# A two-group encoder on one Trainium2 core: a new clock for two interleaved threads, a fixed count of gathered rows ahead of a chain, and a contiguous scatter operand

## The chip, the cores and the metric

The kernel runs on one core of a Trainium2 chip. The metric is the device time of one execution in microseconds (us), lower is better. Engines are named as in the profile: PE (matmuls), DVE (vector), ACT (activations), POOL (which issues the gathers), SP (which issues the weight loads).

## The reference

Two request groups ("prompt" and "sample", 256 tokens each, 1024 features) go through the same two layers. Layer 0 mixes with a three-group attention, layer 1 with a short convolution. Behind the mixer each layer has the PEER channel mixer, which dominates the time:

```python
def block(xc):                                   # 128 tokens
    q = (xc @ w_query).reshape(C, PEER_HEADS, 2, PEER_HALF)
    s = jnp.einsum('chpk,hpnk->chpn', q, sub_keys)
    sv, si = lax.top_k(s, PEER_TOPK)             # 16 of 128 keys, twice
    ...                                          # 16 best of 256 pairs -> eidx, 8 heads x 16
    g = jax.nn.softmax(fv, axis=-1)
    u = u_tab[eidx]                              # rows of a 16384 x 1024 table
    h = jax.nn.gelu(jnp.einsum('chkd,cd->chk', u, xc))
    return jnp.einsum('chk,chkd->cd', (g * h), v_tab[eidx])
...
x = layer_norm(ALPHA * x + f, ln2_gain[i], ln2_bias[i])
x = x + jax.nn.sigmoid(x @ ple_w_gate[i]) * (p[i] @ ple_w_proj[i])
```

## The kernel before

Each group has a generator ("thread"): `thread_a` for the prompt, `thread_b` for the sample. Each `yield` hands back a cost; the thread with the smaller clock runs next, and its clock sets the priority of what it emits (sample's clock starts at `T0B`). A scheduler then writes one instruction order per engine from these priorities and from its own estimates of durations. On the chip every engine goes through its order from front to back, so an instruction that waits holds up all behind it on its engine.

The two groups do PEER in two ways. The prompt **gathers**: for each of 2 token tiles, 8 heads and 16 picks, one indirect DMA fetches 128 rows of the table u (`gather`, L472, issued by POOL), and DVE multiplies them with x and sums (L489); then the same for table v (L510). That is 512 such row tiles a layer ("rows" below), in a ring of 8 buffers (`GB`). When the last row of tile 1 is in, DVE adds the residual and normalises (`done`), PE transposes the result (`transpose_x`, L139), and the gate (`ple`) follows, then the prompt's next layer.

The sample goes **densely** through all 16384 experts: 64 pairs of blocks, for each a load of 1 MB of u (`dense_u`, L528), 16 matmuls `hid`, a gelu on ACT (L556), a product with the gate matrix G on DVE (`hs`, L557), 1 MB of v (L559) and 8 matmuls `out` (L102). For the first 8 pairs (`pre`) `hid` is done ahead, during the sample's routing. G is built by `scatter`, in 8 chunks of 16 blocks: DVE compares (L587) and multiplies (L589) to one-hot rows I0 in float16, and PE multiplies them with the float8 matrix J, one small matmul a token (L596 in chunk 0, L603 in the others).

The sample's chain from its routing to the end of chunk 0 is kept free of rows: `hold[0]` is set when the sample's routing starts (L803), and the prompt then emits no row until chunk 0 is emitted; the next 16 rows' DVE work stands behind the last L589 of that chunk.

Of the kernel before, what the change touches and what calls it, by code (L numbers as in the profile page):

```python
# [46 lines left out]
def encoder_trunk(ctx: ExitStack, tc: tile.TileContext, A: dict):  # L47
# [11 lines left out]
    n_ = [0]  # L59
    hold = [False, None, 0]  # L60

# [22 lines left out]
    iota = T(cp, [P, NC_], "iota")  # L84
    iota16 = T(cp, [P, CH, 2 * TG], "iota16", F16)
    iotaj = T(cp, [P, NK // 4], "iotaj", F16)
# [45 lines left out]

    def transpose_x(e, x, xt, natural=False):
        for t in range(NT):
            for half in range(2):
                pt = e.tr([4, P])
                for j in range(4):
                    kc = half * 4 + j
                    nc.tensor.transpose(pt[:, j], x[t][:, kc * P:(kc + 1) * P], ident)  # L139
# [49 lines left out]
    def attention(e, g, x):  # L189
# [13 lines left out]
        def project(hp):  # L203
            base = (hp // 2) * 9 + (0 if hp % 2 == 0 else 5)
            qkT = T(ap, [P, NG, 4, S], "qkT", bufs=2)
            for gr in range(NG):
                ps = token_major(e, xt, "w_qkv", base + gr)
                for t in range(NT):
# [13 lines left out]
                    nc.scalar.activation(qkT[:, gr, :, t * P:(t + 1) * P], pt, AF.Copy)  # L222
                yield 11
            v01 = T(ap, [P, NT, 2, 2, HD], "v01", bufs=2)
            ps = token_major(e, xt, "w_qkv", base + 3)
            for t in range(NT):
                nc.scalar.activation(v01[:, t].rearrange("p a b d -> p (a b d)"), ps[t], AF.Copy)
            yield 11
            if hp % 2 == 0:
                v2 = T(ap, [P, NT, 4, HD], "v2", bufs=2)  # L230
                ps = token_major(e, xt, "w_qkv", base + 4)
                for t in range(NT):
                    nc.scalar.activation(v2[:, t].rearrange("p a d -> p (a d)"), ps[t], AF.Copy)
                yield 11
            else:
# [3 lines left out]
        def attend(hp):  # L239
# [35 lines left out]
            for hh in range(2):  # L275
                for t in range(NT):
                    held.append((hh, t, scores(hh, t)))
                    if len(held) > AHEAD:
                        values(*held.pop(0))
                    yield 2.5  # L280
            for z in held:
# [22 lines left out]
        out_proj(e, x, ot, "w_out", (ps, steps))  # L304
        yield 22

# [168 lines left out]
    def peer_gather(i, x, sel, done):  # L475
# [6 lines left out]
        def up(t, h):  # L482
            dots = T(sp, [P, TOPK], "dots", bufs=2)
            for k in range(TOPK):
                while hold[0]:
                    yield 1.0
                r = gather(u, index(t, h * TOPK + k))
                with held():
# [8 lines left out]
        def down(t, h):  # L497
# [3 lines left out]
            for k in range(TOPK):  # L501
                while hold[0]:
                    yield 1.0
                r = gather(v, index(t, h * TOPK + k))
                c = cf[:, k:k + 1]
# [38 lines left out]
    def peer_dense(e, i, xt, sel, spill, newx, pre):  # L544
# [32 lines left out]
        def scatter(c):  # L577
# [3 lines left out]
            for tg in range(S // TG):  # L581
                ts = slice(tg * TG, (tg + 1) * TG)
                if tg % 2 == 0:
                    t2 = slice(tg * TG, (tg + 2) * TG)
                    I1 = T(dp, [P, CH, 2 * TG], "I1", F16, bufs=1)
                    I0w = T(dp, [P, 2 * CH * 2 * TG], "I0", F16, bufs=2).rearrange("p (q a b) -> p q a b", q=2, a=CH)
                    nc.vector.tensor_tensor(I1, iota16, ic[:, t2].unsqueeze(1).to_broadcast([P, CH, 2 * TG]), op=ALU.is_equal)  # L587
                    bc = [P, 2, CH, 2 * TG]
                    last = nc.vector.tensor_tensor(I0w, I1.unsqueeze(1).to_broadcast(bc), gT[:, :, t2].unsqueeze(2).to_broadcast(bc), op=ALU.mult)  # L589
                I0 = I0w[:, :, :, (tg % 2) * TG:(tg % 2 + 1) * TG]  # L590
                ps = T(e.phid, [P, 512], "hid").rearrange("p (a q b) -> p a q b", q=2, b=CH)
                gv = G[:, :, ts]
                if c < SCU:
                    for k in range(TG):
                        for q in range(2):
                            nc.tensor.matmul(ps[:, k, 0], J[:, tg * TG + k], I0[:, q, :, k], start=q == 0, stop=q == 1)  # L596
                    nc.scalar.activation(gv, ps[:, :, 0].rearrange("p a b -> p b a"), AF.Copy)
                    if tg == S // TG - 1:
                        hold[:] = [False, last.ins, 2 * GB]
                    yield G  # L600
                    continue
                for k in range(TG):
                    nc.tensor.matmul(ps[:, k], J[:, tg * TG + k], I0[:, :, :, k], start=True, stop=True)  # L603
                nc.scalar.activation(gv, ps[:, :, 0].rearrange("p a b -> p b a"), AF.Copy)  # L604
# [33 lines left out]
    def ple(e, g, i, x, which):  # L638
# [4 lines left out]
        if which:  # L643
            norms(e, which, i, x)
        xt = transpose_x(e, x, e.xt())
        for nb in range(2):
# [93 lines left out]

    GCOST = 6.0
    T0B = 280.0
    RCOST = 21.0
    PM = -10000.0
# [34 lines left out]
    def thread_b():  # L779
# [4 lines left out]
        for i in range(DEPTH):  # L784
# [55 lines left out]
def _layout(inputs):  # L840
# [84 lines left out]
```

## Time and profile before

| | us |
|---|---|
| median of 3 runs (lowest to highest) | 3628.53 (3628.45 to 3635.97) |
| the profiled execution, its own time | 3627.66 |
| span of its instructions | 3625.9 |
| around the span | 1.8 |

Mean granted TensorE clock 0.955 of full speed. Busy shares are averages over stages with different limits; the stages are read from windows and waits further down.

### The profile page before, as it was taken

How to read it: one execution, taken by the hardware profiler on the slowest of the kernel's cores; microseconds unless marked ns; L12 is line 12 of the kernel's file. 1: busy time of each engine (PE TensorE's matmuls, PEld its weight loads, DVE VectorE, ACT ScalarE, POOL GpSimd, SP SyncE). 2: the span in 40 equal slices, each digit the busy share in tenths (PEclk: the TensorE clock that was granted, in tenths of full speed). 3: DMA queues.
4: the chain of work that ended last, by engine and by line, in shares of the span. 5: the costliest groups of instructions: out<-in, count | busy, mean ns of one | idle time of the engine just before them, and what ended most of it. 6: DMA issues, size and time to landing. Idle time of an engine off the chain costs nothing. (4 is left out here: it accounts for less than half of the span.)

```text
span 3625.9 us, 42260 instructions
## 1 busy us (share of the span) xinstructions
PE 3335.0 (92%) x15472; PEld 2229.4 (61%) x15472; DVE 2197.1 (61%) x4766; ACT 554.6 (15%) x1374; POOL 1400.5 (39%) x1476
## 2 busy tenths in 40 slices
PE   9998999988699999999999859895999999999967
PEld 4555555567366677667666647584566676666633
DVE  0002796047977777777741265468877777676683
ACT  1222223223100001000001112122000001000001
POOL 0110574000355555555620041000655555555660
PEclk9999999989699999999999979996999999999988
DMA  6433797333499999999974565442999999999993
GB/s 213 136 117 128 276 347 269 116 131 128 170 363 376 382 378 378 376 379 378 393 304 142 165 211 176 142 142 80 370 364 380 385 378 375 377 374 372 405 410 124
DMA packets 243568, 1007.14 MB, mean 278 GB/s; under 512 B 27553, under 2 KB 28961, under 8 KB 210593
## 3 DMA queue, kind: packets, MB, share of 16 engines
q0 software_dynamic: 147456, 536.94, 39.1%
q1 hardware_dynamic: 87264, 448.83, 34.2%
q10 hardware_dynamic: 8640, 18.68, 1.4%
q8 instruction: 122, 2.00, 0.2%
q14 instruction: 86, 0.70, 0.1%
HBM read 999.09 MB, written 5.24 MB: 277 GB/s over the span
## 5 line engine op out<-in xcount | busy, mean ns | idle before, releaser
L472 POOL DMA_INDIRECT g<-in_u_dram,ei x512 | 640.3, 1251 | 531.5 <-DVE g L489 201.1
L102 PE MATMUL out<-ur,hs 128*128 128x512 f32 x1824 | 811.6, 598 | 31.1 <-ACT k L653 28.1
L102 PE MATMUL hid<-bx1T,ur 128*128 128x256 f32 x3584 | 800.8, 382 | 11.5 <-DVE G L605 11.4
L472 POOL DMA_INDIRECT g<-in_v_dram,ei x512 | 625.7, 1222 | 424.4 <-DVE acc L510 164.1
L102 PEld LDWEIGHTS hid<-bx1T,ur 128*128 128x128 f32 x3584 | 682.3, 192 | 129.2 <-issue 26.8
L510 DVE SCALAR_TENSOR_TENSOR acc<-g,cf,acc 128x1024 f32<-128x1024 f32 x508 | 651.8, 1283 | 46.5 <-DMA g<-in_v_dram,ei 34.9
L489 DVE SCALAR_TENSOR_TENSOR g<-g,xa 128x1024 f32<-128x1024 f32 x512 | 605.9, 1223 | 47.3 <-DMA g<-in_u_dram,ei 46.5
L102 PEld LDWEIGHTS out<-ur,hs 128*128 128x128 f32 x1824 | 342.5, 192 | 417.1 <-issue 383.2
L102 PE MATMUL mm<-raw,x 128*128 128x512 f32 x1280 | 568.1, 595 | 10.1 <-DMA x<-in_xT_dram 8.1
L102 PEld LDWEIGHTS mm<-raw,x 128*128 128x128 f32 x1280 | 237.3, 191 | 272.5 <-issue 267.9
L557 DVE SCALAR_TENSOR_TENSOR hs<-hs,G 128x512 f32<-128x512 f32 x112 | 77.8, 694 | 315.8 <-ACT hs L556 315.8
L250 DVE SCALAR_TENSOR_TENSOR k<-tr,mask 128x512 f32<-128x512 f32 x32 | 22.0, 687 | 401.9 <-PE tr L247 401.9
L603 PEld LDWEIGHTS <-J 128*128 128x128 fp8e4 x3584 | 216.7, 113 | 53.7 <-issue 40.3
L102 PE MATMUL out<-bx1T,ur 128*128 128x256 f32 x1024 | 231.8, 388 | 17.0 <-ACT k L369 11.0
L603 PE MATMUL hid<-I,J 128*128 128x32 f16 x3584 | 229.5, 233 | 6.0 <-DVE G L605 6.0
L102 PEld LDWEIGHTS out<-bx1T,ur 128*128 128x128 f32 x1024 | 198.3, 195 | 47.1 <-ACT k L369 13.5
L556 ACT ACTIVATE hs<-hid 128x512 f32<-128x512 f32 x112 | 66.9, 597 | 1038.6 <-PE hid L102 1038.5
L400 POOL TENSOR_TENSOR ci<-sif 128x32 f32<-128x32 f32 x64 | 17.4, 292 | 534.9 <-ACT sif L386 533.2
L102 PE MATMUL out<-ur,x 128*128 128x512 f32 x448 | 207.2, 619 | 12.2 <-DVE x L557 12.2
L214 POOL TENSOR_TENSOR rm<-k,rope 128x128 f32<-128x128 f32 x48 | 26.1, 544 | 432.4 <-ACT k L210 432.2
L589 DVE TENSOR_TENSOR I<-I,gT 128x1024 f16<-128x1024 f16 x128 | 88.4, 691 | 135.0 <-PE hid L603 125.8
L604 ACT ACTIVATE G<-hid 128x256 f32<-128x256 f32 x224 | 85.9, 383 | 528.1 <-PE hid L603 527.8
(182 smaller groups left out, 2641.5 us busy)
## 6 DMA issues: line engine op xcount, KB each, us to landing
ur<-in_uT_dram SPq DMA_DIRECT2D x128, 1024.0 KB, 8.2
ur<-in_vp_dram SPq DMA_DIRECT2D x128, 1024.0 KB, 8.2
raw<-in_w_qkv_dram SPq DMA_DIRECT2D x144, 512.0 KB, 4.4
raw<-in_w_q_dram SPq DMA_DIRECT2D x32, 512.0 KB, 3.7
ur<-in_w_q_dram SPq DMA_DIRECT2D x32, 512.0 KB, 3.5
raw<-in_c_in_dram SPq DMA_DIRECT2D x24, 512.0 KB, 3.6
ur<-in_c_in_dram SPq DMA_DIRECT2D x24, 512.0 KB, 3.6
raw<-in_w_out_dram SPq DMA_DIRECT2D x16, 512.0 KB, 4.3
```

What stands on the lines that cost most here:

```text
L102: nc.tensor.matmul(out, a, b, start=first, stop=last)
L214: nc.gpsimd.tensor_tensor(m1, st[:, :, :2 * RH], c, op=ALU.mult)
L250: nc.vector.scalar_tensor_tensor(prf, sc, SCALE, mask[:, t], op0=ALU.mult, op1=ALU.add)
L400: eng.tensor_tensor(dst[:, :, off:off + n], src[:, :, 1, 0:n], src[:, :, 0, a0:a0 + 1].to_broadcast([P, 2, n]), op=ALU.add)
L472: nc.gpsimd.indirect_dma_start(out=t, out_offset=None, in_=tab, in_offset=bass.IndirectOffsetOnAxis(ap=idx, axis=0))
L489: nc.vector.scalar_tensor_tensor(r, r, 1.0, x[t], op0=ALU.mult, op1=ALU.mult, accum_out=dots[:, k:k + 1])
L510: nc.vector.scalar_tensor_tensor(acc[t], r, c, acc[t], op0=ALU.mult, op1=ALU.add)
L556: nc.scalar.activation(hs, hid, AF.Gelu)
L557: nc.vector.scalar_tensor_tensor(hs, hs, 1.0 / GSC, G[:, 2 * pr:2 * pr + 2], op0=ALU.mult, op1=ALU.mult)
L589: last = nc.vector.tensor_tensor(I0w, I1.unsqueeze(1).to_broadcast(bc), gT[:, :, t2].unsqueeze(2).to_broadcast(bc), op=ALU.mult)
L603: nc.tensor.matmul(ps[:, k], J[:, tg * TG + k], I0[:, :, :, k], start=True, stop=True)
L604: nc.scalar.activation(gv, ps[:, :, 0].rearrange("p a b -> p b a"), AF.Copy)
```

## The change

Five edits. (1) Rows ahead of the sample's chain: the flag is replaced by a count. A layer's first `CAP[i]` rows (170 in layer 0, 100 in layer 1) may be emitted whenever the prompt's clock says so; all further ones wait until chunk 0 of that layer's scatter is emitted. (2) The costs that the threads yield: `T0B` 280 to 420, `RCOST` 21 to 26, `GCOST` 6.0 to 5.2, the attention's projections 11 to 17, its score steps 2.5 to 5, its end 22 to 35. (3) The prompt's gate transposes start with tile 1, and those of tile 0 stand behind the first of tile 1. (4) I0 and I1 are laid out with the 16 block indices innermost, so the scatter matmul's moving operand is 32 neighbouring float16 values instead of 32 values that lie 64 bytes apart; DVE's second inputs (`ic`, `gT`) are then broadcast along the innermost axis instead of an outer one. (5) The iota constant follows that layout.

```diff
-    hold = [False, None, 0]
+    hold = [0, None, 0]
+    rows = [0]
...
-    iota16 = T(cp, [P, CH, 2 * TG], "iota16", F16)
+    iota16 = T(cp, [P, 2 * TG, CH], "iota16", F16)
...
-        for t in range(NT):
+        lead = None
+        for t in reversed(range(NT)) if late else range(NT):
...
+                    with tc.issue_after(lead) if lead is not None and t == 0 else nullcontext():
+                        ins = nc.tensor.transpose(pt[:, j], x[t][:, kc * P:(kc + 1) * P], ident)
+                    if late and lead is None:
+                        lead = ins.ins
...
-                yield 11
+                yield PCOST
...
-                while hold[0]:
+                while rows[0] >= CAP[i] and hold[0] <= i:
                     yield 1.0
+                rows[0] += 1
...
-                    nc.vector.tensor_tensor(I1, iota16, ic[:, t2].unsqueeze(1).to_broadcast([P, CH, 2 * TG]), op=ALU.is_equal)
-                    bc = [P, 2, CH, 2 * TG]
-                    last = nc.vector.tensor_tensor(I0w, I1.unsqueeze(1).to_broadcast(bc), gT[:, :, t2].unsqueeze(2).to_broadcast(bc), op=ALU.mult)
+                    nc.vector.tensor_tensor(I1, iota16, ic[:, t2].unsqueeze(2).to_broadcast([P, 2 * TG, CH]), op=ALU.is_equal)
+                    bc = [P, 2 * TG, 2, CH]
+                    last = nc.vector.tensor_tensor(I0w, I1.unsqueeze(2).to_broadcast(bc), gT[:, :, t2].rearrange("p q b -> p b q").unsqueeze(3).to_broadcast(bc), op=ALU.mult)
...
-                    nc.tensor.matmul(ps[:, k], J[:, tg * TG + k], I0[:, :, :, k], start=True, stop=True)
+                    nc.tensor.matmul(ps[:, k].rearrange("p q b -> p (q b)"), J[:, tg * TG + k], I0[:, k].rearrange("p q a -> p (q a)"), start=True, stop=True)
...
-        xt = transpose_x(e, x, e.xt())
+        xt = transpose_x(e, x, e.xt(), late=not e.deep)
...
-    GCOST = 6.0
-    T0B = 280.0
-    RCOST = 21.0
+    CAP = (170, 100)
+    GCOST = 5.2
+    T0B = 420.0
+    RCOST = 26.0
+    PCOST = 17.0
...
-            hold[0] = True
```

Where the new order differs, in three places. First DVE at the end of the sample's attention in layer 0 (`y` is the sample's state, `lnst`/`lnmv` its layer norm, `g` a gathered row, `xa` the prompt's state). Before:

```order
L187 SCALAR_TENSOR_TENSOR y_427_1681<-y_427_1681,mm_3840 128x512
L160 BN_STATS lnst_3940<-y_427_1681 128x6
L187 SCALAR_TENSOR_TENSOR y_427_1681<-y_427_1681,mm_3868 128x512
L160 BN_STATS lnst_3940<-y_427_1681 128x6
L161 BN_AGGR lnmv_3939<-lnst_3940 128x2
L174 SCALAR_TENSOR_TENSOR y_427_1681<-y_427_1681,lnmv_3939,raw_3935 128x1024
```

The same place in the changed kernel (L495 is the old L489):

```order
L192 SCALAR_TENSOR_TENSOR y_365_1413<-y_365_1413,mm_4107 128x512
L495 SCALAR_TENSOR_TENSOR g_4172,dots_4147<-g_4172,xa_5_98 128x1024
L165 BN_STATS lnst_4216<-y_365_1413 128x6 x2
L495 SCALAR_TENSOR_TENSOR g_4175,dots_4147<-g_4175,xa_5_98 128x1024
L495 SCALAR_TENSOR_TENSOR g_4178,dots_4147<-g_4178,xa_5_98 128x1024
L166 BN_AGGR lnmv_4215<-lnst_4216 128x2
```

Rows now stand between the steps of the sample's layer norm; in DVE's whole order 76 rows stood ahead of it before, and now 152 do, with 18 more between its first and the routing's first instruction.

Second, PE at the gate transposes of the prompt's tile 1 in layer 0 (`av`), inside the sample's dense stage. Before:

```order
L102 MATMUL out_5121<-ur_12232,hs_12229 128x512
L139 MATMUL av_10684<-ident_75,xa_6_99 128x128 x4
L139 MATMUL av_10690<-ident_75,xa_6_99 128x128 x2
L102 MATMUL out_5118<-ur_12444,hs_12441 128x512
L102 MATMUL out_5119<-ur_12444,hs_12441 128x512
```

Changed (L142 is the old L139, L611 the old L603):

```order
L611 MATMUL hid_10762<-I_2208_10759,J_5416 128x32
L142 MATMUL av_9482<-ident_75,xa_6_99 128x128 x4
L142 MATMUL av_9488<-ident_75,xa_6_99 128x128 x4
L611 LDWEIGHTS J_5416
L611 MATMUL hid_10781<-I_2208_10759,J_5416 128x32
```

They moved forward from the last pair of the dense stage to its middle, between two scatter groups. Counted in the order from the first matmul of chunk 0 to these transposes, PE now has 512 matmuls of 16 columns, 1392 of 32, 576 of 256 and 344 of 512; before 512, 1792, 896 and 504. In layer 1 it has 512, 1664, 704 and 416; before 512, 1792, 896 and 516.

Third, PE at the start of the prompt's convolution in layer 1 (`av<-x,raw` 128x256). Before:

```order
L139 MATMUL av_10956<-ident_75,xa_6_99 128x128 x4
L102 MATMUL av_10968<-x_10928,raw_10969 128x256 x8
L102 MATMUL av_10981<-x_10928,raw_10982 128x256 x8
L102 MATMUL av_11000<-x_10928,raw_11001 128x256 x8
L102 MATMUL av_11088<-x_10928,raw_11089 128x256 x8
```

Changed:

```order
L142 MATMUL av_9766<-ident_75,xa_6_99 128x128 x4
L103 MATMUL hid_11842<-bx1T_4244,ur_11843 128x256 x4
L103 MATMUL av_9778<-x_9738,raw_9779 128x256 x4
L103 MATMUL hid_11842<-bx1T_4244,ur_11843 128x256 x3
L103 MATMUL av_9778<-x_9738,raw_9779 128x256 x4
L103 MATMUL av_9791<-x_9738,raw_9792 128x256 x8
```

The convolution stood behind the sample's dense matmuls and now stands among them (`hid<-bx1T,ur`).

## Rows read from the trace of the kernel before

**Rows 1.** The page: span, busy time of each engine, and the DMA's GB/s over 40 slices of 90.6 us.
```profile
span 3625.9 us, 42260 instructions
...
PE 3335.0 (92%) x15472; PEld 2229.4 (61%) x15472; DVE 2197.1 (61%) x4766; ACT 554.6 (15%) x1374; POOL 1400.5 (39%) x1476
...
GB/s 213 136 117 128 276 347 269 116 131 128 170 363 376 382 378 378 376 379 378 393 304 142 165 211 176 142 142 80 370 364 380 385 378 375 377 374 372 405 410 124
```

**Rows 2.** Waits of PE over the whole span: instruction waiting, who ended the wait, total us, times, longest.
```profile
PE av L139 <- DVE xa L175: 55.5, 2, 45.0
PE hid L459 <- DVE k L449: 41.0, 2, 20.8
PE hid L596 <- DVE I L589: 39.7, 2, 19.8
PE out L102 <- ACT k L653: 28.1, 1, 28.1
PE av L102 <- ACT k L369: 13.8, 1, 13.8
```

**Rows 3.** Stretches: length, busy us of PE, PEld, DVE, ACT, POOL (instructions), granted clock, DMA share, GB/s.
```profile
587.00:757.00 170.00, 157.77 (x547) 85.65 (x546) 40.56 (x81) 45.78 (x103) 19.93 (x45) 0.98 0.35 113
...
1100.00:1800.00 700.00, 697.77 (x3553) 485.30 (x3552) 507.42 (x735) 67.79 (x153) 405.79 (x329) 1.00 0.98 380
...
2560.00:2600.00 40.00, 40.00 (x206) 21.57 (x204) 32.03 (x47) 3.07 (x8) 28.32 (x23) 1.00 1.02 410
...
2700.00:3300.00 600.00, 597.77 (x3041) 415.93 (x3040) 436.28 (x637) 58.78 (x133) 346.35 (x279) 0.99 0.98 375
...
3400.00:3480.00 80.00, 80.00 (x277) 52.51 (x276) 53.46 (x70) 3.80 (x7) 50.65 (x41) 1.00 1.02 413
...
3505.00:3550.00 45.00, 0.09 (x1) 0.00 (x0) 42.72 (x42) 3.96 (x16) 20.27 (x19) 0.52 0.73 289
```

**Rows 4.** The row gathers alone (L472): POOL's busy us and their number in each stretch, granted clock, DMA share and GB/s of all transfers.
```profile
390.00:595.00 205.00, 99.21 (x84) 1.00 0.94 351
940.00:1870.00 930.00, 530.39 (x428) 0.98 0.96 371
2100.00:2200.00 100.00, 34.62 (x28) 0.78 0.65 226
2500.00:3550.00 1050.00, 601.71 (x484) 0.95 0.94 363
```

**Rows 5.** Timeline of PE, from several windows: start us, us, instructions merged, idle time before them. An instruction of 4-byte operands is shown as two matmuls.
```profile
756.84 3.68 PE L139 MATMUL tr<-ident,y 128*128 128x128 f32 x16 [6.78 <-DVE y L175]
...
939.07 10.67 PE L596 MATMUL hid<-I,J 128*128 128x16 f16 x393 [19.84 <-DVE I L589]
...
1206.20 7.07 PE L102 MATMUL hid<-bx1T,ur 128*128 128x256 f32 x32
1213.11 1.07 PE L603 MATMUL hid<-I,J 128*128 128x32 f16 x16
1214.00 7.10 PE L102 MATMUL out<-ur,hs 128*128 128x512 f32 x16
...
1899.93 0.82 PE L139 MATMUL av<-ident,xa 128*128 128x128 f32 x6
...
2521.10 13.87 PE L596 MATMUL hid<-I,J 128*128 128x16 f16 x512 [19.84 <-DVE I L589]
...
3482.83 13.90 PE L102 MATMUL out<-ur,hs 128*128 128x512 f32 x32
...
3550.09 1.97 PE L139 MATMUL av<-ident,xa 128*128 128x128 f32 x8 [45.00 <-DVE xa L175]
```

**Rows 6.** Costliest groups of DVE by shape: busy us, mean ns of one.
```profile
L510 DVE SCALAR_TENSOR_TENSOR acc<-g,cf,acc 128x1024 f32<-128x1024 f32 x508 | 651.8, 1283 | 46.5 <-DMA g<-in_v_dram,ei 34.9
...
L489 DVE SCALAR_TENSOR_TENSOR g<-g,xa 128x1024 f32<-128x1024 f32 x512 | 605.9, 1223 | 47.3 <-DMA g<-in_u_dram,ei 46.5
...
L589 DVE TENSOR_TENSOR I<-I,gT 128x1024 f16<-128x1024 f16 x128 | 88.4, 691 | 135.0 <-PE hid L603 125.8 <-PE hid L596 5.7
...
L587 DVE TENSOR_TENSOR I<-iota,ic 128x512 f16<-128x512 f16 x128 | 53.9, 421 | 0.5
...
L572 DVE TENSOR_TENSOR I<-iotaj,jT 128x1024 f16<-128x1024 f16 x16 | 18.8, 1214 | 0.1
```

**Rows 7.** What DVE waited for from 1000 to 1860 us.
```profile
DVE hs L557 <- ACT hs L556: 148.3, 47, 6.0
DVE I L589 <- PE hid L603: 63.5, 25, 4.0
DVE acc L510 <- DMA g<-in_v_dram,ei: 15.5, 14, 2.0
```

**Rows 8.** DMA: the gathers' queue (packets, MB, share of 16 engines), and the dense stage's two weight loads (count, KB each, us to landing).
```profile
q0 software_dynamic: 147456, 536.94, 39.1%
...
ur<-in_uT_dram SPq DMA_DIRECT2D x128, 1024.0 KB, 8.2
ur<-in_vp_dram SPq DMA_DIRECT2D x128, 1024.0 KB, 8.2
```

**Rows 9.** Timeline of DVE behind the last row of layer 1.
```profile
3539.60 1.22 DVE L514 SCALAR_TENSOR_TENSOR xa<-xa,acc 128x1024 f32<-128x1024 f32 x1
```

More of the change, by code (lines that the diff above doesn't have):

```diff
@@ L131, in col_major, with transpose_x @@
         return ps
-    def transpose_x(e, x, xt, natural=False):
-        for t in range(NT):
+    def transpose_x(e, x, xt, natural=False, late=False):
+        lead = None
+        for t in reversed(range(NT)) if late else range(NT):
             for half in range(2):
@@ L138, in transpose_x @@
                     kc = half * 4 + j
-                    nc.tensor.transpose(pt[:, j], x[t][:, kc * P:(kc + 1) * P], ident)
+                    with tc.issue_after(lead) if lead is not None and t == 0 else nullcontext():
+                        ins = nc.tensor.transpose(pt[:, j], x[t][:, kc * P:(kc + 1) * P], ident)
+                    if late and lead is None:
+                        lead = ins.ins
                 if not natural:
@@ L227, in project @@
                 nc.scalar.activation(v01[:, t].rearrange("p a b d -> p (a b d)"), ps[t], AF.Copy)
-            yield 11
+            yield PCOST
             if hp % 2 == 0:
@@ L233, in project @@
                     nc.scalar.activation(v2[:, t].rearrange("p a d -> p (a d)"), ps[t], AF.Copy)
-                yield 11
+                yield PCOST
             else:
@@ L279, in attend @@
                         values(*held.pop(0))
-                    yield 2.5
+                    yield 5.0
             for z in held:
@@ L304, in attention @@
         out_proj(e, x, ot, "w_out", (ps, steps))
-        yield 22
+        yield 35
     def conv(e, x):
@@ L501, in down @@
             for k in range(TOPK):
-                while hold[0]:
+                while rows[0] >= CAP[i] and hold[0] <= i:
                     yield 1.0
+                rows[0] += 1
                 r = gather(v, index(t, h * TOPK + k))
@@ L517, in peer_gather @@
         cfs, acc = {}, {}
+        rows[0] = 0
         yield 0.0
@@ L584, in scatter @@
                     t2 = slice(tg * TG, (tg + 2) * TG)
-                    I1 = T(dp, [P, CH, 2 * TG], "I1", F16, bufs=1)
-                    I0w = T(dp, [P, 2 * CH * 2 * TG], "I0", F16, bufs=2).rearrange("p (q a b) -> p q a b", q=2, a=CH)
-                    nc.vector.tensor_tensor(I1, iota16, ic[:, t2].unsqueeze(1).to_broadcast([P, CH, 2 * TG]), op=ALU.is_equal)
-                    bc = [P, 2, CH, 2 * TG]
-                    last = nc.vector.tensor_tensor(I0w, I1.unsqueeze(1).to_broadcast(bc), gT[:, :, t2].unsqueeze(2).to_broadcast(bc), op=ALU.mult)
-                I0 = I0w[:, :, :, (tg % 2) * TG:(tg % 2 + 1) * TG]
+                    I1 = T(dp, [P, 2 * TG, CH], "I1", F16, bufs=1)
+                    I0w = T(dp, [P, 2 * CH * 2 * TG], "I0", F16, bufs=2).rearrange("p (b q a) -> p b q a", q=2, a=CH)
+                    nc.vector.tensor_tensor(I1, iota16, ic[:, t2].unsqueeze(2).to_broadcast([P, 2 * TG, CH]), op=ALU.is_equal)
+                    bc = [P, 2 * TG, 2, CH]
+                    last = nc.vector.tensor_tensor(I0w, I1.unsqueeze(2).to_broadcast(bc), gT[:, :, t2].rearrange("p q b -> p b q").unsqueeze(3).to_broadcast(bc), op=ALU.mult)
+                I0 = I0w[:, (tg % 2) * TG:(tg % 2 + 1) * TG]
                 ps = T(e.phid, [P, 512], "hid").rearrange("p (a q b) -> p a q b", q=2, b=CH)
@@ L595, in scatter @@
                         for q in range(2):
-                            nc.tensor.matmul(ps[:, k, 0], J[:, tg * TG + k], I0[:, q, :, k], start=q == 0, stop=q == 1)
+                            nc.tensor.matmul(ps[:, k, 0], J[:, tg * TG + k], I0[:, k, q], start=q == 0, stop=q == 1)
                     nc.scalar.activation(gv, ps[:, :, 0].rearrange("p a b -> p b a"), AF.Copy)
                     if tg == S // TG - 1:
-                        hold[:] = [False, last.ins, 2 * GB]
+                        hold[:] = [hold[0] + 1, last.ins, 2 * GB]
                     yield G
@@ L887, in _layout @@
     put("ident", np.eye(P, dtype=np.float32))
-    put("iota16", np.repeat(np.arange(CH, dtype=np.float16), 2 * TG)[None])
+    put("iota16", np.tile(np.arange(CH, dtype=np.float16), 2 * TG)[None])
     put("iotaj", np.arange(NK // 4, dtype=np.float16)[None])
```

## The prediction

> **What bounds the kernel now.** I read the busy shares first, then PE's waits, then stretches, then the gathers by stretch. PE is busy 92% of the span [rows 1]. It is not one limit throughout. In the long dense stretches PE is full (698 of 700 us) and the DMA, which carries the sample's weights and the prompt's gathered rows together, runs at 375 to 380 GB/s [rows 3]. That is not the DMA's own limit: where there is more to fetch it moves 410 and 413 GB/s in the same kind of work, with PE just as full [rows 3]. In that stretch DVE is busy 507 of 700 us and waits mostly for PE and ACT, hardly for rows (15.5 us against 148.3 and 63.5) [rows 7]. So there PE sets the pace and the rows follow it. PE idles around the chains: 20 us before each layer's index transposes (L459) and 20 before each chunk 0 (L596), 28.1 and 13.8 in the prompt's serial stretch near 2000 to 2200 us, and 55.5 for the prompt's normalised state, 45.0 of it behind the last gather of layer 1 [rows 2, 5].
>
> I cut the span at four instructions of PE's order: first matmul of chunk 0 and gate transposes of tile 1, in each layer. The rows give 939.07, 1899.93, 2521.10 and 3550.09 us [rows 5], so five stages A to E of 939, 961, 621, 1029 and 76 us.
>
> **The price of PE's work.** From the timeline [rows 5]: a matmul of 256 columns is two passes of 6.91/32 = 0.216 us, so 0.432; one of 512 columns two passes of 0.429, so 0.858 (32 passes in 13.90, the last one's tail taken off). A scatter matmul of 16 columns takes 13.87/512 = 0.027, one of 32 columns 0.89/16 = 0.056 (1213.11 to 1214.00). By these the counts before give 933 us for B and 944 for D. The rows show 961, and 984 up to the 45 us wait: 28 and 40 us of waits and slow clock at the stage's start, which I keep.
>
> **Scatter matmul (edit 4).** Both shapes load the same kind of J, yet time goes with the columns: 0.027 for 16, 0.056 for 32. So loading J takes at most 0.027, and a column that lies 64 bytes from the next costs 1.75 ns. The nearest row with neighbouring values is the 256-column pass, 0.84 ns a column: 32 make 0.027. I take 0.027 for the 32 columns. Bounds: 0.056, if distance isn't what costs, and 0.013, if a 2-byte column costs half of that pass's. There are 1792 a layer, so the gain is 52 us of PE a layer, 0 to 77.
>
> **One-hot rows on DVE (edit 4).** The new second operands repeat along the innermost axis. The trace has that form: L572, float16, 1024 elements, takes 1214 ns where L589 takes 691 [rows 6]. I take 1.21 for the multiply and, with half the elements, 0.68 for the compare (now 0.42): +0.78 us for each of 64 groups, 50 us of DVE a layer. The bound below is no change. [...]
> What hides the 50 us is DVE's idle 193 of 700 [rows 3]. Per pair of the changed B, counted below, DVE would have 8 rows at 1.25 (10.0 us), about 2.1 of other work (96 us beside the rows' 411 in 45 pairs) and 0.9 more: 13 us of a pair's 15.4. It fits, with little to spare; without that cover the 50 us would be on the path.
>
> **Rows ahead of the chain (edits 1 and 2).** Before, 84 gathers are issued ahead of chunk 0 in layer 0 and 28 in layer 1 (8 of each wait in the buffers), and 428 and 484 follow [rows 4]. With the count, 170 and 100 rows are consumed and 8 more are waiting, so 334 and 404 follow. The 94 extra rows of layer 0 fall into 587 to 757 us, where DVE is busy 41 of 170 us and the DMA moves 113 GB/s [rows 3]: 94 x 1.25 = 118 us of DVE fit, and 49 MB at some 270 GB/s of free rate need 182 us, just about. But the order puts the last 18 of them between the steps of the sample's layer norm, for which PE already waits 6.8 us [rows 5]. 12 to 13 of those 18 at 1.2 us stand ahead of its last step: **A grows by 15 us to 954** (0 to 45). In layer 1 the 80 extra rows go beside the sample's dense end and its gate.
>
> **B and D.** The gate transposes, and all of PE behind them, now stand in the middle of the dense stage, and cannot run until all 512 rows are in. So B is the longer of two times.
> PE: 512 x 0.027 + 1392 x 0.027 + 576 x 0.432 + 344 x 0.858 = 595, with the 28 of its start 623. In D 720, with 40 it is 760.
> DMA: a row is 536.94 MB/1024 = 0.524 MB, a weight load 1.049 MB [rows 8]. B needs 334 rows (175 MB) and 36 + 43 loads (83 MB), together 258 MB; D 404 rows and 44 + 52 loads, 313 MB. When PE no longer holds the rows back, the 410 to 413 GB/s should nearly be reached; I take 404. That is 639 and 775 us, and 23 around it: 12 until the first gather moves, 10.5 from the last row's end to the transposes (3539.60 to 3550.09 [rows 5, 9]).
> **B = 665, D = 800**, set by the rows, with PE waiting some 40 us in each. Before, the same sum gives 887 us for layer 0 (349 MB), below PE's 961, as observed.
>
> **C.** By the same prices PE has 786 us there (498 before), since the rest of the dense stage, the prompt's gate, convolution and routing all fall into it. Before, C was 123 us longer than its work. The 28.1, the 13.8 and the 10.5 that is left of the 55.5 go, because dense matmuls now stand between the prompt's steps: 71 stay. I add 40: the prompt's routing now shares DVE with the dense products, and the sample's norm, gate and convolution lose the prompt's work that filled their gaps. **C = 897.**
>
> **E.** PE has 245 us behind the transposes (70 before) and I add 15 of waits: **260**.
>
> The late tile-1 transposes (edit 3) cost 8 matmuls, 1.8 us, inside B and D. Edit 5 costs nothing (one load).
>
> **Sum.** 954 + 665 + 897 + 800 + 260 = 3576, and 1.8 around the span: 3578. The profiled execution took 3627.66, the median of the runs is 3628.53, so no correction is needed.
>
> **Rivals.**
> *The DMA stays at 380 GB/s* (rows, weights and busier DVE never let it reach 410). Then B = 679 + 23 = 702 and D = 824 + 23 = 847: 3578 + 37 + 47 = 3662, slower than before. For it: 1300 us of trace run at 375 to 380 [rows 3]. Against: PE was full there. It decides from 390 GB/s downwards: there B and D together lose the 50 us. Chance 0.20.
> *The rows keep up with PE.* Then B = 623, D = 760: 3578 - 82 = 3496. It needs 258 MB in 600 us, 430 GB/s; the highest row is 413. Chance 0.10. [...]
> *The scatter matmul doesn't get faster.* Then PE has 42 us more in B (665, no change), 50 in D (810), 12 in C, 4 in E: 3604. Chance 0.08.
> *The early rows delay the sample's chain.* If DVE falls behind in 587 to 757 us, A grows by 45 and the gate of layer 1 by 15 more: 3623. Chance 0.12.
>
> **Numbers.** My forecast has 0.50, with a range of its own of 3540 to 3615. The predicted time is **3578**. About 0.2% (7 us) is what a measurement can tell from no change. Faster: 0.50 + 0.10 + 0.08, less 0.01 for their upper edge, 0.67. Same: most of the last rival, 0.09. Slower: the DMA rival and the rest, 0.24. The range, 3505 to 3660, leaves out the low end of the second rival and half of the first.
>
> **What would show it.** Scatter matmuls of 32 columns 0.027 apart; L595 and L597 at 0.68 and 1.21; 178 and 108 gathers ahead of the two chunks 0; the DMA above 395 GB/s in the dense stretches, with DVE waiting for rows; PE waiting for the prompt's state in the middle of both dense stages; and no PE idle time in the prompt's convolution. Wrong it would be if the DMA stays at 380, if PE waits for DVE all through the dense stages, or if the routing of the sample starts more than 30 us later.

## The result and the profile after

| | before | after |
|---|---|---|
| median (lowest to highest), us | 3630.24 (3628.45 to 3635.97) | 3662.19 (3657.11 to 3669.28) |
| ratio, 95% interval | 1 | 1.0088 (1.0072 to 1.0104) |
| span of the profiled execution | 3625.9 | 3667.5 |

The change makes the kernel 0.9% slower; 3578 was forecast, and 3662 lies just outside the range. The profiled execution is the longest of the four, so the stage sums below stand some 7 us above the median.

Rows of the changed kernel. First the page: span, and busy time of each engine.

```profile
span 3667.5 us, 42272 instructions
PE 3289.7 (90%) x15472; PEld 2157.5 (59%) x15472; DVE 2280.7 (62%) x4766; ACT 569.5 (16%) x1387; POOL 1446.7 (39%) x1476
```

PE has 45 us less work than before [rows 1] and a span 42 us longer. The next view is PE's time line at the cuts between the stages (start, length, what ran; in brackets the idle time ahead and what ended it).

```profile
785.79 3.67 PE L142 MATMUL tr<-ident,y 128*128 128x128 f32 x16 [12.65 <-DVE y L180]
802.87 2.47 PE L103 MATMUL out<-bx1T,ur 128*128 128x256 f32 x5 [13.41 <-DMA ur<-in_w_q_dram]
975.42 3.86 PE L604 MATMUL hid<-I,J 128*128 128x16 f16 x128 [20.64 <-DVE I L597]
1680.77 1.08 PE L142 MATMUL av<-ident,xa 128*128 128x128 f32 x8
2574.18 3.86 PE L604 MATMUL hid<-I,J 128*128 128x16 f16 x128 [20.64 <-DVE I L597]
3419.81 0.82 PE L142 MATMUL av<-ident,xa 128*128 128x128 f32 x6
```

| stage | A | B | C | D | E |
|---|---|---|---|---|---|
| before [rows 5] | 939 | 961 | 621 | 1029 | 76 |
| forecast | 954 | 665 | 897 | 800 | 260 |
| measured | 975 | 705 | 893 | 846 | 248 |

C and E came within 12 us of the forecast; the miss is 40 us in B, 46 in D and 21 in A. The gate transposes stand in mid-stage with no idle time ahead of them: the prompt's rows were in on time, though not by much (DVE's last step on the prompt's state ends 6 us ahead of them in layer 0 and 14 in layer 1). PE's waits say where the time is (engine, line, what it waited for: total us, times, longest).

```profile
PE hid L103 <- DVE G L613: 131.5, 77, 3.0
PE hid L604 <- DVE I L597: 43.4, 14, 20.6
...
PE hid L611 <- DVE G L613: 14.9, 7, 4.9
```

The first row is the dense loop's `hid` group waiting for DVE's add into G (L613, the old L605). In the page's groups (busy us, mean ns of one, idle time before) `hid` and the scatter matmuls were, before,

```profile
L102 PE MATMUL hid<-bx1T,ur 128*128 128x256 f32 x3584 | 800.8, 382 | 11.5 <-DVE G L605 11.4
...
L603 PE MATMUL hid<-I,J 128*128 128x32 f16 x3584 | 229.5, 233 | 6.0 <-DVE G L605 6.0
```

and after,

```profile
L103 PE MATMUL hid<-bx1T,ur 128*128 128x256 f32 x3584 | 856.4, 399 | 131.5 <-DVE G L613 131.5
...
L611 PE MATMUL hid<-I,J 128*128 128x32 f16 x3584 | 116.6, 177 | 17.6 <-DVE G L613 14.9 <-DVE I L597 2.4 <-ACT hs L564 0.3
```

So PE has 45 us less work and 87 more idle time: 129 more of waits for G (131.5 + 14.9 against 11.4 + 6.0) and, on balance, 42 less elsewhere; the 45.0 at the last transposes [rows 5] is among what went. In stage B the waits for G are 65 us, in D 81. Stretches (length, busy PE, PEld, DVE, ACT, POOL, granted clock, DMA share, GB/s):

```profile
1000.00:1660.00 660.00, 594.69 (x3119) 391.38 (x3118) 539.68 (x723) 60.21 (x138) 416.03 (x330) 0.95 0.98 383
2700.00:3300.00 600.00, 540.91 (x2798) 363.66 (x2797) 483.23 (x651) 53.51 (x123) 386.31 (x307) 0.96 1.00 391
```

PE is busy 90%, and its mean granted clock is 0.95 and 0.96. Before, it was busy 99.7% from 1100 to 1800 us and 99.6% from 2700 to 3300, at 1.00 and 0.99 [rows 3]. DVE's forms:

```profile
L597 DVE TENSOR_TENSOR I<-I,gT 128x1024 f16<-128x1024 f16 x128 | 156.6, 1223 | 206.9 <-PE hid L611 205.4
L595 DVE TENSOR_TENSOR I<-iota,ic 128x512 f16<-128x512 f16 x128 | 87.7, 685 | 0.5
L613 DVE TENSOR_TENSOR G<-G,hid 128x256 f32<-128x256 f32 x224 | 85.3, 413 | 23.4 <-ACT G L612 23.4
```

Last, one pair of blocks in the loop, first PE (`hid`, the scatter matmuls L611, `out`):

```profile
1201.79 8.86 PE L103 MATMUL hid<-bx1T,ur 128*128 128x256 f32 x32 [2.65 <-DVE G L613]
1210.48 0.20 PE L611 MATMUL hid<-I,J 128*128 128x32 f16 x2
1210.54 7.11 PE L103 MATMUL out<-ur,hs 128*128 128x512 f32 x16
1217.49 0.91 PE L611 MATMUL hid<-I,J 128*128 128x32 f16 x30
1220.04 8.86 PE L103 MATMUL hid<-bx1T,ur 128*128 128x256 f32 x32 [1.65 <-DVE G L613]
...
1238.29 7.17 PE L103 MATMUL hid<-bx1T,ur 128*128 128x256 f32 x32 [1.65 <-DVE G L613]
```

and DVE in the same pair:

```profile
1218.43 1.23 DVE L597 TENSOR_TENSOR I<-I,gT 128x1024 f16<-128x1024 f16 x1 [2.99 <-PE hid L611]
1219.57 0.41 DVE L613 TENSOR_TENSOR G<-G,hid 128x256 f32<-128x256 f32 x1
...
1221.05 0.42 DVE L613 TENSOR_TENSOR G<-G,hid 128x256 f32<-128x256 f32 x1
```

DVE in a pair of the kernel before, and the start of PE's next `hid` group there:

```profile
1214.63 0.42 DVE L605 TENSOR_TENSOR G<-G,hid 128x256 f32<-128x256 f32 x1
...
1222.05 0.69 DVE L589 TENSOR_TENSOR I<-I,gT 128x1024 f16<-128x1024 f16 x1 [1.84 <-PE hid L603]
1222.66 0.41 DVE L605 TENSOR_TENSOR G<-G,hid 128x256 f32<-128x256 f32 x1
```

```profile
1221.84 7.14 PE L102 MATMUL hid<-bx1T,ur 128*128 128x256 f32 x32
```

Before, PE ran 16 scatter matmuls, `out` and 16 more ahead of the next `hid`, and DVE added the first group's half to G while `out` ran (1214.00 [rows 5], 1214.63), ahead of the multiply. Now 30 of the 32 scatter matmuls stand behind `out`, right ahead of `hid`, and DVE has the multiply ahead of both adds. It waits 2.99 us for those scatter matmuls to have read their rows, takes 1.23, and only then comes the add (1219.57). The tile `hid` has two PSUM buffers, which `hid` groups and scatter groups share, so the next `hid` group starts when the first scatter group is copied and added: 1.65 us late. In this pair its 32 matmuls then take 8.86 us instead of 7.07 [rows 5]. Not every wait does that: of the 77 `hid` groups that waited for G, 29 took 8.86 us or more and 48 took 7.17, as the one at 1238.29. The pair shown takes 18.25 us from `hid` to `hid`, where it took 15.64 (1206.20 to 1221.84). Over 1000 to 1700 us the median step is 16.57 us, and 15.7 before.

### The profile page after: what moved, and what is told of

It is laid out like the page before. It is cut to its first block, busy times and chain, and to the rows that moved or that the text cites. A ratio compares the mean times of both kernels' runs of the same rounds, so it can differ in the third digit from the quotient of the medians.

```text
span 3667.5 us, 42272 instructions
## 1 busy us (share of the span) xinstructions
PE 3289.7 (90%) x15472; PEld 2157.5 (59%) x15472; DVE 2280.7 (62%) x4766; ACT 569.5 (16%) x1387; POOL 1446.7 (39%) x1476
## 4 chain that ended last, share of the span: by engine, by line
PE 66%; DVE 16%; issue 9%; DMA 4%; POOL 3%; ACT 1%; ACTq 0%; POOLq 0%; SPq 0%; DVEq 0%
PE out L103 24%; PE hid L103 20%; PE mm L103 12%; PE av L103 5%; DVE g L495 3%; POOL g L477 3%; DMA g<-in_u_dram,ei 2%; PE hid L611 2%; DVE I L597 1%; DVE acc L517 1%; DVE k L423 1%; DMA g<-in_v_dram,ei 1%; DVE k L421 1%; DVE si L362 1%; DVE si L356 1%
## 5 line engine op out<-in xcount | busy, mean ns | idle before, releaser
L103 PE MATMUL hid<-bx1T,ur 128*128 128x256 f32 x3584 | 856.4, 399 | 131.5 <-DVE G L613 131.5
L103 PEld LDWEIGHTS hid<-bx1T,ur 128*128 128x128 f32 x3584 | 709.3, 200 | 254.4 <-DVE G L613 139.4
L477 POOL DMA_INDIRECT g<-in_u_dram,ei x512 | 657.0, 1283 | 431.6 <-DVE acc L517 152.2
L103 PE MATMUL out<-ur,hs 128*128 128x512 f32 x1824 | 811.0, 597 | 15.1 <-DVE k L666 6.7
L495 DVE SCALAR_TENSOR_TENSOR g<-g,xa 128x1024 f32<-128x1024 f32 x512 | 611.6, 1223 | 49.4 <-DMA g<-in_u_dram,ei 48.9
L597 DVE TENSOR_TENSOR I<-I,gT 128x1024 f16<-128x1024 f16 x128 | 156.6, 1223 | 206.9 <-PE hid L611 205.4
L103 PEld LDWEIGHTS out<-bx1T,ur 128*128 128x128 f32 x1024 | 197.6, 195 | 55.0 <-issue 13.8
L611 PEld LDWEIGHTS <-J 128*128 128x128 fp8e4 x3584 | 114.4, 96 | 86.0 <-issue 76.2
L103 PE MATMUL av<-x,raw 128*128 128x256 f32 x640 | 147.9, 388 | 9.8 <-ACT k L374 9.8
```

The source lines that it names most:

```text
L103: nc.tensor.matmul(out, a, b, start=first, stop=last)
L477: nc.gpsimd.indirect_dma_start(out=t, out_offset=None, in_=tab, in_offset=bass.IndirectOffsetOnAxis(ap=idx, axis=0))
L495: nc.vector.scalar_tensor_tensor(r, r, 1.0, x[t], op0=ALU.mult, op1=ALU.mult, accum_out=dots[:, k:k + 1])
L597: last = nc.vector.tensor_tensor(I0w, I1.unsqueeze(2).to_broadcast(bc), gT[:, :, t2].rearrange("p q b -> p b q").unsqueeze(3).to_broadcast ...
L611: nc.tensor.matmul(ps[:, k].rearrange("p q b -> p (q b)"), J[:, tg * TG + k], I0[:, k].rearrange("p q a -> p (q a)"), start=True, stop=True)
```

## The experiments

Each ratio is to the kernel before, timed on the same chip. "Edits 1 to 3" are the count, the planner's numbers and the late transposes, "edits 4 and 5" the contiguous operand. The time lines give A to E.

| kernel | median us | ratio to before (95%) | A, B, C, D, E |
|---|---|---|---|
| e1 operand alone | 3695.7 | 1.0185 (1.0168 to 1.0202) | 939, 884, 757, 1028, 85 |
| e2 after without operand | 3662.1 | 1.0089 (1.0072 to 1.0106) | 971, 758, 889, 960, 85 |
| e3 after, adds first | 3592.4 | 0.9899 (0.9882 to 0.9915) | 974, 729, 879, 922, 85 |
| e4 after, sum on PE | 3678.3 | 1.0133 (1.0116 to 1.0150) | 973, 752, 929, 937, 85 |
| e5 after, token pairs | 3576.8 | 0.9854 (0.9838 to 0.9870) | 972, 722, 882, 913, 85 |
| e6 = e3 with 76 and 20 rows | 3609.2 | 0.9944 (0.9927 to 0.9960) | 949, 926, 661, 994, 76 |
| e8 = e1, adds first | 3566.8 | 0.9821 (0.9804 to 0.9837) | 942, 927, 628, 996, 76 |
| e9 before, token pairs | 3548.4 | 0.9776 (0.9760 to 0.9793) | 938, 919, 623, 990, 77 |
| e10 = e9 with edit 1 | 3581.5 | 0.9858 (0.9841 to 0.9874) | 963, 724, 888, 919, 86 |
| e11 = e9 with edit 2 | 3613.7 | 0.9947 (0.9930 to 0.9963) | 969, 746, 882, 780, 232 |
| e13 = e10 with 76 and 100 rows | 3545.8 | 0.9758 (0.9742 to 0.9774) | 941, 929, 674, 922, 86 |
| e14 = e10 with 76 and 60 rows | 3530.2 | 0.9719 (0.9702 to 0.9735) | 939, 922, 653, 933, 79 |

The theory called "loop" says that the slow multiply and the order that comes with it hold PE; the rival called "DMA" that the transfers set B and D, as the prediction had it.

**e1, the operand alone**, is the kernel before with edits 4 and 5 as the diff of the change shows them.

> The kernel before with the contiguous scatter operand alone (edits 4 and 5); count of rows, planner numbers and gate transposes as before. Theory loop (the broadcast one-hot multiply of 1.22 us makes DVE reach the G add late, and PE's next hid group waits for that add): PE shows the wait hid <- DVE G in both dense stages, over 80 us where the kernel before has 11, and the time is within 0.5% of before although PE saves some 90 us of scatter matmul. Theory DMA (the transfer rate of about 390 GB/s set stages B and D of the changed kernel, and DVE's share doesn't matter): here the rows are late by nothing, PE set the pace in the kernel before, so the operand alone saves 60 to 100 us (3530 to 3570).

The waits of PE:

```profile
PE hid L102 <- DVE G L605: 154.4, 93, 3.3
```

The edit that should have gained 50 us a layer costs 66 by itself. The mechanism is the one of "loop"; its size was underrated (1.9% slower, not equal). "DMA" expected 3530 to 3570 and is out here.

**e2, the change without the operand**, takes the same lines back in the changed kernel.

> The changed kernel without edits 4 and 5: the scatter operand is strided as before, the rest of the change stands. Theory loop: the wait hid <- DVE G falls from 131 us to under 30, the slowed hid groups go with it, and the PE pays 90 us more for scatter matmuls in exchange: time 3600 to 3665, B about 665 to 705 by PE's own work. Theory DMA: B and D stay at 705 and 846 within 10 us, so that the time is within 0.5% of the changed kernel. Theory schedule (the 36 us by which chunk 0 of layer 0 starts late come from the rows taken ahead): A stays 970 or more.

The wait falls to 9.1 us, and the `hid` matmuls to 383 ns from 399. The time doesn't move, since PE pays 112 us for the strided scatter matmuls (228.7 against 116.6) and the prompt's routing now waits without cover:

```profile
PE av L103 <- ACT k L374: 67.8, 2, 42.2
PE out L103 <- ACT k L661: 47.2, 1, 47.2
PE hid L103 <- DVE G L613: 9.1, 9, 1.1
```

B and D are 53 and 114 us longer than in the changed kernel, outside both theories' figures, but they are no measure here: the gate transposes moved. In layer 0 more dense work stands ahead of them (672 matmuls of `hid` from chunk 0 on, where the changed kernel has 576), and in layer 1 they went back to the end of the dense stage (E 85). A is 971, as the theory "schedule" has it. But a time that equals the changed kernel's tells the theories apart only through its waits. So the next one decides.

**e3, adds first**, the changed kernel with

```diff
-                    last = nc.vector.tensor_tensor(I0w, ...)
+                    with tc.issue_after(gadd[0]) if gadd[0] is not None else nullcontext():
+                        last = nc.vector.tensor_tensor(I0w, ...)
...
-                nc.vector.tensor_tensor(gv, gv, ps[:, :, 1]..., op=ALU.add)
+                gadd[0] = nc.vector.tensor_tensor(gv, gv, ps[:, :, 1]..., op=ALU.add).ins
```

> The changed kernel with one edit: DVE's one-hot multiply of a pair of scatter groups stands behind both G adds of the groups before it, as the only change of order that is asked for. Theory loop: PE's wait hid <- DVE G falls from 131 us to under 40, B and D fall by 25 to 45 us each towards 665 and 800, and the time to 3580 to 3620. Theory DMA: the wait goes but PE then waits elsewhere in the stage, or at the gate transposes for the last rows; B and D stay within 10 us of 705 and 846, the time within 0.5% of the changed kernel.

Its waits, its stretches, and the same place of the loop:

```profile
PE av L103 <- ACT k L374: 65.0, 2, 39.3
PE out L103 <- ACT k L664: 47.0, 1, 47.0
...
PE hid L103 <- DVE G L616: 6.2, 10, 1.5
```

```profile
1000.00:1660.00 660.00, 641.99 (x3533) 424.08 (x3532) 541.71 (x737) 63.66 (x154) 422.45 (x326) 0.99 1.00 392
2700.00:3300.00 600.00, 590.03 (x3227) 398.01 (x3226) 481.51 (x656) 57.85 (x140) 370.43 (x290) 1.00 1.00 394
```

```profile
1194.12 0.56 PE L614 MATMUL hid<-I,J 128*128 128x32 f16 x16
1194.52 7.11 PE L103 MATMUL out<-ur,hs 128*128 128x512 f32 x16
1201.47 0.55 PE L614 MATMUL hid<-I,J 128*128 128x32 f16 x16
1201.88 7.15 PE L103 MATMUL hid<-bx1T,ur 128*128 128x256 f32 x32
...
1203.02 0.41 DVE L616 TENSOR_TENSOR G<-G,hid 128x256 f32<-128x256 f32 x1
1203.35 1.21 DVE L600 TENSOR_TENSOR I<-I,gT 128x1024 f16<-128x1024 f16 x1
```

One asked-for change of place takes 70 us off. DVE does the same work (541.71 and 481.51 us against 539.68 and 483.23), the multiply is as slow, and the DMA moves a little more (392 and 394 GB/s). "DMA" is out. Two things limit the reading. The order of PE followed the edit too: the scatter groups stand apart again, and the gate transposes stand where they do in e2. So B and D rose where "loop" had them falling, and by themselves are no measure. And the prompt's routing lost its dense cover (65.0 and 47.0 us of waits in these two places, against 9.8 and none in the changed kernel), so the edit by itself may well be worth more than 70 us.

**e4, the sum on PE**, lets every chunk do what chunk 0 does:

```diff
-                if c < SCU:
+                if True:
                     for k in range(TG):
                         for q in range(2):
                             nc.tensor.matmul(ps[:, k, 0], J[:, tg * TG + k], I0[:, k, q], start=q == 0, stop=q == 1)
...
-                    if tg == S // TG - 1:
+                    if c == 0 and tg == S // TG - 1:
```

> The changed kernel with the two halves of a group summed by TensorE in every chunk (two 16-column matmuls a token into one PSUM region, as chunk 0 has it), so that the G add on DVE is gone (224 adds of some 0.35 us) and a group's PSUM buffer comes free after ACT's copy. Price on PE: 3584 more matmuls of 0.027 us, 97 us in all, minus the 0.027 to 0.056 of the old ones. Theory loop: PE's wait for DVE G is zero, the clock in the dense windows goes to 0.99, and B and D change by less than 25 us, because PE's added work takes the place of the wait. Theory DMA: with DVE freed of 80 us, B and D stay within 10 us of 705 and 846 as well; the two are told apart by e3, and here by whether DVE waits for rows (over 60 us in a 500 us window if the DMA sets the pace, under 15 if not).

No wait for G is left, PE is busy without a gap (660.00 of 660, 600.00 of 600) at clock 1.00, and the kernel is slower by 16 us: the scatter matmuls went from 147 to 235 us (8192 of 16 columns) and the routing waits 108.5 and 46.2 us without cover. DVE waits for rows only 9.6 us in the first stretch and 12.0 in the second, which is the answer of "loop". B and D grew by 47 and 91 us, more than forecast; the gate transposes moved as in e2 (688 matmuls of `hid` ahead of them in B, E 85).

**e5, token pairs**, a third layout in the changed kernel; it splits the multiply into one instruction for each half q:

```diff
-                    I1 = T(dp, [P, 2 * TG, CH], "I1", F16, bufs=1)
+                    I1 = T(dp, [P, TG, CH, 2], "I1", F16, bufs=1)
...
+                    bc = [P, TG, CH, 2]
+                    for q in range(2):
+                        last = nc.vector.tensor_tensor(I0w[:, :, q], I1, gT[:, q, t2].rearrange("p (b z) -> p b z", z=2).unsqueeze(2).to_broadcast(bc), op=ALU.mult)
...
+                    nc.tensor.matmul(ps[:, k]..., J[:, tg * TG + k], I0[:, k // 2, :, :, k % 2]..., start=True, stop=True)
```

> The changed kernel with a third layout of the scatter operand: two neighbouring tokens innermost, so that the broadcast operands of DVE run along a middle axis and TensorE's 32 columns lie 4 bytes apart. The one-hot multiply becomes two instructions of 512 elements. Theory loop, the price of the one-hot multiply as its cause: if the pair layout gives DVE back its faster rate, the multiplies take 0.35 to 0.40 us each instead of 1.22 in one, the compare 0.42 instead of 0.68, DVE gets some 45 us a layer back, PE's wait hid <- DVE G falls from 131 us to under 40, and the time to 3560 to 3610. If DVE doesn't return to the faster rate, the two take 0.65 each, and the wait stays over 100 us unless the order on DVE changes. TensorE's 32 columns: 0.025 us if 4 bytes cost nothing, 0.056 if any distance does.

```profile
L598 DVE TENSOR_TENSOR I<-I,gT 128x512 f16<-128x512 f16 x256 | 98.3, 420 | 74.7 <-PE hid L612 69.9 <-PE hid L605 4.7
L595 DVE TENSOR_TENSOR I<-iota,ic 128x512 f16<-128x512 f16 x128 | 53.4, 417 | 0.5
L612 PE MATMUL hid<-I,J 128*128 128x32 f16 x3584 | 121.5, 177 | 24.2 <-ACT hs L564 16.1 <-DVE G L614 7.3 <-DVE I L598 0.6
```

Both sides are had: DVE's faster rate (417 ns for the compare, 2 x 420 for the multiply) and PE's fast matmul. The wait for G is 7.8 us without any order asked for, and the time 85 us under the changed kernel's.

**e6, e3 with fewer rows ahead**: `CAP = (76, 20)` in place of (170, 100).

> The kernel with the one-hot multiply behind the G adds (3592 us), and the count of rows ahead of chunk 0 set to 76 and 20, which is what was consumed there before (edit 1 undone in its size). Theory rows: the 36 us by which chunk 0 of layer 0 stands later than before come from the 94 rows taken ahead; A falls from 974 to 939 to 948, the wait of the y transposes from 12.6 to under 7.5 us, and the rows fit into the dense stage, so that the time is 3550 to 3575. Rival clock: A comes from the planner's numbers (edit 2) and stays above 965; the time is then 3585 to 3610, or more if the added rows hold B back.

A fell to 949 and the wait ahead of the y transposes to 6.78 us, so 25 of A's 36 us are the rows', and about 10 the planner's numbers'. The time went the other way, up by 17. That is above the range of "rows" and in the range of its rival, whose A (over 965) failed: fewer rows ahead put the wait for the last gate transposes back (45.2 us).

**e8, the kernel before with the operand and adds first**, e1 with e3's edit.

> The kernel before with the contiguous operand (edits 4 and 5, which alone gave 3695.7 us) and the one-hot multiply behind the G adds; count of rows, planner numbers and gate transposes as before. Theory loop: the wait hid <- DVE G falls from 154 us to under 30, TensorE's hid matmuls from 399 to about 382 ns, and the time by 130 to 180 us, to 3515 to 3565. Theory that edits 1 to 3 are needed for the operand to pay (the prompt's serial end without cover): the wait goes, but the time stays above 3600, with the wait of the gate transposes for the prompt's state back at 40 us or more at the end of the dense stages.

The wait is 6.4 us, `hid` 381 ns, the time 129 us under e1's: the same edit as in e3, here with no change in the cover of the routing. It ends 2 us above what "loop" gave, with 46.4 us of wait at the last gate transposes.

**e9, the kernel before with token pairs**, e5's edit alone.

> The kernel before with the pair layout of the scatter operand in place of the strided one, and nothing else. Theory loop: with the faster rate on DVE the wait hid <- DVE G stays near the 11 us of before, TensorE saves up to 110 us of scatter matmul, and the time is 3530 to 3580. If DVE does not return to the faster rate, this kernel looks like the contiguous operand alone (3695 us), or, where the order on DVE has the adds earlier, lies between 3560 and 3640.

The forecast of "loop" holds: 3548. One pair of blocks in PE's time line:

```profile
1206.21 7.07 PE L102 MATMUL hid<-bx1T,ur 128*128 128x256 f32 x32
1213.11 0.56 PE L604 MATMUL hid<-I,J 128*128 128x32 f16 x16
1213.52 7.11 PE L102 MATMUL out<-ur,hs 128*128 128x512 f32 x16
1220.47 0.56 PE L604 MATMUL hid<-I,J 128*128 128x32 f16 x16
1220.87 4.35 PE L102 MATMUL hid<-bx1T,ur 128*128 128x256 f32 x19
```

This pair takes 14.66 us; others take 15.1 to 15.2, and the median step from 1000 to 1700 us is 15.1, against 15.7 before and 16.57 after.

**e10 and e11, edits 1 and 2 apart** on e9.

> The kernel before with the pair layout (3548 us) and edit 1: the count of 170 and 100 rows ahead of chunk 0, with the planner numbers and the gate transposes of before. Three layouts of the operand agree that edits 1 to 3 together cost 25 to 33 us. Theory count: the rows taken ahead delay stage A (937 to 965 or more) and bring nothing back, so the time is 3565 to 3585. Rival (from the kernel with the count set back, which got slower by 17 us although A shrank by 25): the rows ahead shorten the wait of the last gate transposes for the prompt's state (50.3 us) and pay for themselves; the time is 3520 to 3550.

> The kernel before with the pair layout (3548 us) and edit 2: the planner's numbers of the changed kernel, with the old rule for the rows ahead of chunk 0 and the gate transposes of before. Theory clock: the new numbers set the prompt's routing and norm of layer 1 where no dense matmul covers them, so that stage C grows from 623 to 655 or more and the waits for the routing's ACT copies from 14 to over 50 us; the time is 3575 to 3600. Theory count: the numbers alone change less than 10 us (3540 to 3558).

The count alone costs 33 us, the time that the theory "count" gave (it did bring something back: the 50 us wait of the last gate transposes is gone); the planner's numbers alone cost 65, more than either theory had; with edit 3 the three together cost 28 (e5 against e9). They aren't additive: each alone puts the prompt's layer-1 routing where it waits (45.8 and 59.8 us in e10, 67.5 and 46.2 in e11, 13.8 and 29.6 in e9). Nor is e11 free of rows: under the old rule the new numbers let 164 rows pass ahead of chunk 0 in layer 0 and 144 in layer 1 (counted in DVE's trace; e9 has 76 and 20, e10 170 and 100). So the two runs don't price rows and numbers apart; A, at 963 and 969, shows both.

**e13 and e14, the count in layer 1 alone.**

> The kernel before with the pair layout (3548 us) and the count of edit 1 at 76 and 100 rows: layer 0 as before, layer 1 with the 80 more rows ahead of chunk 0. Theory layer 0 (what the count of 170 and 100 costs, 33 us, comes from layer 0: stage A by 26 us, and the prompt's routing in stage C without dense matmuls beside it by 60; layer 1 alone gains): A stays 937 to 943, C within 25 us of 623, the 50 us wait of the last gate transposes goes, and the time is 3480 to 3520. Rival: the 80 rows of layer 1 cost as much in C as they bring in D, and the time stays within 0.5% of 3548 or above.

> The same with 76 and 60 rows. Theory layer 0: half of the gain of 76 and 100, so that the last gate transposes wait 10 to 30 us for the prompt's state and the time is 3500 to 3535. Rival: no gain, 3540 or more.

With 100 rows the 50 us wait goes and D shrinks by 68, but C grows by 51, two thirds of it in new waits of the sample's convolution for ACT (40.8 us against 7.0), and the time is the rival's. With 60 rows C grows by 30 and D shrinks by 57, and the time is in the theory's range. In both the prompt's routing waits as in e9 (13.8 and 29.6 us in e13), so its longer waits in e10 come with the count of layer 0. Of 20, 60 and 100 rows in layer 1, 60 is the best. e14 is the fastest kernel of the study, 2.8% under before.

## Why the prediction was wrong

**The step that failed** is "What hides the 50 us is DVE's idle 193 of 700", with its close "It fits, with little to spare". The prices were right: 1223 and 685 ns against 1.21 and 0.68, and DVE was busy no more than 82% of the stretch (539.68 of 660). But idle time is cover only for work that nothing waits for. Behind the multiply on DVE stood the add into G, PE's next `hid` group waited for that add through a ring of two buffers, and the order that the scheduler writes moved with the operand on both engines: the add behind the multiply, most of the first scatter group behind `out` (e1 has the same with nothing else changed: 26 of 32 scatter matmuls stand behind `out`).

That order could be read in the changed program; the prediction counted matmuls up to the gate transposes and left out the order within one pair of the loop. It named "PE waits for DVE all through the dense stages" among the signs of being wrong, but no rival priced it. The price was 129 us of waits and 56 us of slower `hid` matmuls, against 113 us won on the scatter matmuls. e3, e5, e8 and e9 each remove it.

Two things stay open. e3 and e8 moved the order on both engines at once, so which of the two moves holds PE is not shown; nor is it shown that the scheduler's duration for the multiply is what moved them. What is shown is that the multiply's length by itself, with the order mended, is worth little: e8 is 18 us above e9, e1 147.

**"B = 665, D = 800, set by the rows"** failed with it. In the changed kernel no gate transpose waited for a row, and DVE, which would have had to wait for late rows, waited for PE. From 1000 to 1660 us (what waited, for whom: total us, times, longest):

```profile
DVE I L597 <- PE hid L611: 74.6, 31, 3.3
...
DVE g L495 <- DMA g<-in_u_dram,ei: 5.9, 4, 4.6
DVE acc L517 <- DMA g<-in_v_dram,ei: 3.6, 5, 1.5
```

PE's own sums, 623 and 760, came nearer the cause: with the 65 and 81 us of waits for G and some 26 and 28 of slower `hid` (an estimate, from `hid`'s busy time per matmul before and after) they give 714 and 869, against 705 and 846. The DMA moved 383 and 391 GB/s here, 392 and 394 in e3, 399 and 395 in e5, nowhere over such a stretch the 404 of the sum; and that sum's terms add to 662 and 798. Whether B would come to 665 without the waits no run shows, because the mended kernels have another order. The DMA rival's 3662 is the measured time, and its 702 and 847 are nearly the measured B and D, but its mechanism isn't there: DVE hardly waits for rows, and e3 is 70 us faster at nearly the same rate. A number that fits is no evidence for its mechanism.

**Scatter matmul**: right. 0.027 us forecast; 16 of 32 neighbouring columns take 0.40 us in e3 (1194.12 to 1194.52), 0.025 each.

**A**: +15 forecast, within 0 to 45, +36 measured. The mechanism was right only in part. The wait that was to grow by 15, that of the y transposes, grew by 5.9 (12.65 us instead of 6.78). 23 us come earlier, ahead of that wait, for the planner's numbers and the rows alike, and 8 behind it: the load of w_q is waited for 13.41 us instead of 5.86 before. By e6, 25 of the 36 are the rows' and 10 the numbers'.

**C and E**: 897 and 260 forecast, 893 and 248 measured, and for the reason given: PE was busy 796 and 242 us there, against 786 and 245 in the sums. That the prompt's routing is hidden there holds only for the order of the changed kernel. In e3 and e5, edits 1 to 3 with a mended operand, the same routing waits 112 us. So edits 1 to 3 gain nothing in three of four cases: on the strided operand they cost 33 us (e2), on the contiguous one with adds first 26 (e3 against e8), on pairs 28 (e5 against e9). Only on the contiguous operand as changed do they gain, 33 us (against e1). How much of that is the cover of the routing, and how much the fewer waits in the loop (131 against 154 us), was not separated.

**Edits 3 and 5** were not run alone.

## What to carry to other kernels

Before idle time is called cover, read what stands behind the lengthened instruction on its engine, and who waits for that; where a scheduler writes the order from durations, print one turn of the innermost loop before and after, on both engines. A layout is judged at both ends: here the pair layout gave the reader columns 4 bytes apart (0.026 us a scatter matmul instead of 0.056) and kept most of the writer's rate (2 x 419 ns for a multiply of 1024 elements in e9, 691 in one before), where the contiguous one only moved the cost (0.025 us, and 1223 ns). And when a measured total equals a rival's number, one run that removes the rival's competitor is worth more than the match.

## What the runs showed of the hardware

- Float16 compare and multiply on DVE: 512 elements take 417 to 420 ns with two neighbouring values innermost and the broadcast on a middle axis (e5, e9), 421 with the compare's broadcast on the outer axis [rows 6], and 685 with it innermost (changed kernel, L595); 1024 take 691 with the broadcasts on outer and middle axes [rows 6] and 1223 with one innermost (L597). So in these forms two neighbours were enough. Why the innermost broadcast is slower no run shows.
- Scatter matmuls of 32 columns take 0.026 us with columns 4 bytes apart (e9, 0.41 us for 16), 0.025 with neighbours (e3, 0.40 for 16), and 0.056 with columns 64 bytes apart [rows 5]. No distance in between was run.
- A short wait often cost twice: of the changed kernel's 77 `hid` groups behind a wait for G, most of them of 1.65 us, 29 took 8.86 us or more and 48 took 7.17; no group without a wait took over 7.2. In the slow group at 1220.04 the granted clock is 0.50 from 1221 to 1223 us and 1.00 from 1224; in the group at 1238.29, which took 7.17, it is 1.00 throughout. The mean granted clock of the dense stretches was 0.95 and 0.96, and without the waits (e3) 0.99 and 1.00. What picks the 29 out of the 77 isn't shown.
